# Gated linear attention's recurrence in chunks of 128 tokens instead of 64, decays within a chunk relative to its 64th token

## Chip, core and metric

The kernel runs on one core of a Trainium2 chip. The metric is the device time of one execution in microseconds: 1509.54 us is the median of three runs of the kernel before (1508.78 to 1512.38).

## What is computed

A decoder trunk of two layers on 512 tokens of width 1024. Layer 0 mixes with block-sparse attention and a gated MLP, layer 1 with gated linear attention; each layer then attends to 256 memory tokens and applies a feed-forward part. All inputs and outputs are float32. The change is in layer 1's mixer, with four heads, keys of 128 and values of 256 columns. With b the running sum of the log gates within a chunk, the reference computes it by chunks of 64 tokens:

```python
b = jnp.cumsum(log_a.astype(f32).reshape(Bn, H, nc, GLA_CHUNK, dk), axis=3)
b_last = b[:, :, :, -1:, :]
q_in = qc * jnp.exp(b)
k_in = kc * jnp.exp(-b)
att = jnp.where(causal, jnp.einsum('bhnid,bhnjd->bhnij', q_in, k_in), 0.0)
o_intra = jnp.einsum('bhnij,bhnjv->bhniv', att, vc)
k_state = kc * jnp.exp(b_last - b)
d_state = jnp.einsum('bhnjd,bhnjv->bhndv', k_state, vc)
...
def step(s_prev, xs):
    ds_n, dec_n = xs
    return dec_n[..., None] * s_prev + ds_n, s_prev
...
o_inter = jnp.einsum('bhnid,bhndv->bhniv', q_in, s_before)
```

The chunk's size is a matter of the algorithm only: with another one the sum of o_intra and o_inter is mathematically the same.

## The kernel before

Activations lie transposed, channels on the 128 partitions and 512 tokens along the free axis. Every float32 operand is split into a high half (`split`: a copy to float32r on ScalarE, L109, or with a scale L112) and a low half (the difference on VectorE, L110, or L113), and `mm3` makes each product of three TensorE matmuls: high x high (L132), high x low (L133), low x high (L134). `ws_tile` projects 128 output channels (24 wide matmuls of 512 columns), `gemm_as` projects tokens (L370 to L372).

Layer 1 runs by the tokens of a string, `GLA_ORDER`: z and g make the gates, Q0 to Q3 are `gla_qk` (queries and keys of a head), V0 and V1 the values of two heads, R0 to R3 the output gates, S0 to S3 `gla_core` (scores and recurrence), out the output projection, mem and k the memory keys of the next step. This is the order of the program. A scheduler then orders each engine's queue by its own timeline, so the projections of the next head (wide, into `ps_mm`, four banks) are woven among the narrow matmuls of `gla_core`. On the chip each engine runs its queue in that order.

`gate_decays` makes `bcum`, a scan along the tokens that is set back every 64 (L1378). `gla_qk` scales the queries by exp(b) and the keys by exp(-b), and makes the state's keys, scaled by exp(b_last - b) (`es`, transposed on TensorE by L137). The queries are laid in `qpH`, `qpL` with 64 zero columns between chunks, so that a query-state product over 128 columns of queries touches one chunk's half and adds zeros to the other.

`gla_core` computes the scores by tiles of 128 tokens (key x query, `ps_t`, 128 columns), keeps with `copy_predicated` what the mask `cmi` allows (two blocks of 64 on the diagonal), splits them, and runs eight chunks. An even chunk adds the intra-chunk product of its tile (256 columns); every chunk but the first adds the query-state product (`ps_t<-sH`, `ps_t<-sL`, 256 columns over 128 contraction rows); every chunk but the last makes the key-value product (`ps_s`, 256 columns, over the 64 contraction rows of its half), the new state `st` (L1476, L1478) and its halves `sH`, `sL`. The output is normed, transposed back, gated and split.

## Time and profile before

| | |
|---|---|
| median of three runs | 1509.54 us |
| profiled execution, its own time | 1511.11 us |
| its span, from the first to the last instruction | 1509.4 us |
| busy: TensorE, VectorE, ScalarE | 98%, 70%, 49% |
| mean granted TensorE clock | 0.996 of full speed |
| key-value products of the four heads | from 814.4 to 964 us of the span |

A busy share counts the time in which at least one instruction of the engine is under way. Matmuls are pipelined and their ends are modelled, so TensorE's pace is read from the distance between starts. A bracket in a timeline tells how long the engine was idle and what ended that.

### The profile page before, as it was taken

How to read it: one execution, taken by the hardware profiler on the slowest of the kernel's cores; microseconds unless marked ns; L12 is line 12 of the kernel's file. 1: busy time of each engine (PE TensorE's matmuls, PEld its weight loads, DVE VectorE, ACT ScalarE, POOL GpSimd, SP SyncE). 2: the span in 40 equal slices, each digit the busy share in tenths (PEclk: the TensorE clock that was granted, in tenths of full speed). 3: DMA queues.
4: the chain of work that ended last, by engine and by line, in shares of the span. 5: the costliest groups of instructions: out<-in, count | busy, mean ns of one | idle time of the engine just before them, and what ended most of it. 6: DMA issues, size and time to landing. Idle time of an engine off the chain costs nothing.

```text
span 1509.4 us, 18961 instructions
## 1 busy us (share of the span) xinstructions
PE 1483.3 (98%) x6982; PEld 1213.3 (80%) x6982; DVE 1060.7 (70%) x1873; ACT 742.5 (49%) x1304; POOL 84.5 (6%) x104
## 2 busy tenths in 40 slices
PE   8999999999999999999999999999999999999999
PEld 6787777788888888888687787888888888888877
DVE  6786866755889686786757556867568886877762
ACT  6546553553655353453535434555536553544551
POOL 4511100000000000000000000000000000000000
PEclk9999999999999999999999999999999999999999
DMA  7231331222432432415122222253214325323022
GB/s 218 84 98 57 125 110 58 78 65 68 142 95 77 154 94 88 126 43 162 43 64 77 70 70 70 78 160 112 71 57 145 99 71 160 105 71 119 28 84 98
DMA packets 144269, 143.22 MB, mean 95 GB/s; under 512 B 7532, under 2 KB 105952, under 8 KB 144176
## 3 DMA queue, kind: packets, MB, share of 16 engines
q1 hardware_dynamic: 142272, 140.53, 29.8%
q0 software_dynamic: 800, 1.37, 0.4%
q8 instruction: 55, 0.90, 0.2%
q14 instruction: 38, 0.31, 0.1%
q10 hardware_dynamic: 1104, 0.11, 0.1%
HBM read 139.88 MB, written 2.10 MB: 94 GB/s over the span
## 4 chain that ended last, share of the span: by engine, by line
PE 90%; DVE 3%; ACT 1%; issue 1%; POOL 1%; DMA 0%; ACTq 0%; POOLq 0%
PE ps_mm L132 12%; PE ps_mm L134 12%; PE ps_mm L133 12%; PE ps_mm L370 5%; PE ps_mm L372 5%; PE ps_s L466 5%; PE ps_mm L371 5%; PE ps_s L467 5%; PE ps_s L468 5%; PE ps_t L466 4%; PE ps_t L467 4%; PE ps_t L468 4%; PE ps_t L137 1%; PE ps_mm L137 1%; PE ps_s L132 1%; PE ps_t L132 1%
## 5 line engine op out<-in xcount | busy, mean ns | idle before, releaser
L109 ACT ACTIVATE wh<-raw 128x1024 fp32r<-128x1024 f32 x180 | 190.5, 1058 | 259.3 <-PE ps_mm L133 106.0
L110 DVE TENSOR_TENSOR wl<-raw,wh 128x1024 fp32r<-128x1024 f32 x180 | 221.0, 1228 | 114.5 <-ACT wh L109 106.9
L132 PE MATMUL ps_mm<-slot,wh 128*128 128x512 f32 x544 | 213.0, 396 | 4.0 <-ACT slot L109 2.1
L134 PE MATMUL ps_mm<-slot,wl 128*128 128x512 f32 x544 | 214.6, 395 | 0.0
L133 PE MATMUL ps_mm<-slot,wh 128*128 128x512 f32 x544 | 214.4, 394 | 0.0
L370 PE MATMUL ps_mm<-wh,slot 128*128 128x512 f32 x384 | 151.2, 398 | 2.8 <-DVE slot L900 1.3
L371 PE MATMUL ps_mm<-wh,slot 128*128 128x512 f32 x384 | 151.7, 396 | 0.0
L372 PE MATMUL ps_mm<-wl,slot 128*128 128x512 f32 x384 | 147.1, 394 | 0.1
L466 PE MATMUL ps_s<-wh,slot 128*128 128x512 f32 x320 | 126.4, 395 | 0.8
L467 PE MATMUL ps_s<-wh,slot 128*128 128x512 f32 x320 | 124.9, 390 | 0.0
L132 PEld LDWEIGHTS ps_mm<-slot,wh 128*128 128x128 f32 x544 | 103.1, 190 | 24.6 <-ACT slot L109 2.2
L134 PEld LDWEIGHTS ps_mm<-slot,wl 128*128 128x128 f32 x544 | 103.0, 189 | 21.4
L468 PE MATMUL ps_s<-wl,slot 128*128 128x512 f32 x320 | 119.6, 390 | 0.0
L133 PEld LDWEIGHTS ps_mm<-slot,wh 128*128 128x128 f32 x544 | 102.8, 189 | 20.6
L1237 DVE TENSOR_TENSOR slot<-ps_mm,slot 128x512 f32<-128x512 f32 x80 | 55.1, 690 | 64.4 <-PE ps_mm L134 63.5
L466 PE MATMUL ps_t<-wh,slot 128*128 128x512 f32 x240 | 94.4, 394 | 0.0
L467 PE MATMUL ps_t<-wh,slot 128*128 128x512 f32 x240 | 93.6, 390 | 0.0
L144 POOL TENSOR_TENSOR s<-s,mhalf 128x2 f32<-128x2 f32 (+3 forms) x46 | 52.1, 1135 | 680.3 <-DVE s L142 678.5
L468 PE MATMUL ps_t<-wl,slot 128*128 128x512 f32 x240 | 87.7, 394 | 0.0
L370 PEld LDWEIGHTS ps_mm<-wh,slot 128*128 128x128 f32 x384 | 72.3, 189 | 18.1 <-DVE slot L900 1.7
L372 PEld LDWEIGHTS ps_mm<-wl,slot 128*128 128x128 f32 x384 | 72.2, 188 | 14.5 <-DVE wl L110 0.5
L371 PEld LDWEIGHTS ps_mm<-wh,slot 128*128 128x128 f32 x384 | 72.5, 189 | 13.9
(342 smaller groups left out, 3018.2 us busy)
## 6 DMA issues: line engine op xcount, KB each, us to landing
raw<-in_ffn_w_gu SPq DMA_DIRECT2D x40, 512.0 KB, 3.6
raw<-in_xa_w_kv SPq DMA_DIRECT2D x32, 512.0 KB, 3.8
pt<-in_ffn_w_down SPq DMA_DIRECT2D x64, 256.0 KB, 3.1
raw<-in_od_w_in SPq DMA_DIRECT2D x24, 512.0 KB, 3.6
pt<-in_ffn_w_gu SPq DMA_DIRECT2D x40, 256.0 KB, 3.7
raw<-in_xa_w_q SPq DMA_DIRECT2D x16, 512.0 KB, 3.8
raw<-in_xa_w_out SPq DMA_DIRECT2D x16, 512.0 KB, 3.4
raw<-in_ev_w_in SPq DMA_DIRECT2D x12, 512.0 KB, 4.1
```

The source lines that it names most:

```text
L109: A.activation(h, src, AF.Copy)
L110: V.tensor_tensor(l, src, h.bitcast(F32), ALU.subtract)
L132: PE.matmul(ps, ah, bh, start=start, stop=False)
L133: PE.matmul(ps, ah, bl, start=False, stop=False)
L134: PE.matmul(ps, al, bh, start=False, stop=stop)
L370: PE.matmul(pss[t], a, wh[:, kk, :], start=st, stop=False)
L371: PE.matmul(pss[t], b, wh[:, kk, :], start=False, stop=False)
L372: PE.matmul(pss[t], a, wl[:, kk, :], start=False, stop=sp_)
L466: PE.matmul(acc[t], ah, h[:, i, :], start=st, stop=False, skip_group_check=True)
L467: PE.matmul(acc[t], al, h[:, i, :], start=False, stop=False, skip_group_check=True)
L468: PE.matmul(acc[t], ah, l[:, i, :], start=False, stop=sp_, skip_group_check=True)
L1237: V.tensor_tensor(xT[m], ps, xT[m], ALU.add)
```

## The change

The loop runs over four chunks of 128 tokens, and the scan is set back every 128 tokens. The queries are scaled by exp(b - b at the 64th token) for the scores (`qcH`, `qcL`) and by exp(b) for the state (`q0H`, `q0L`), the keys by exp(b at the 64th token - b) for the scores and by exp(b_last - b) for the state. The decay of the state is a small tile `dec` of four columns. The mask is a whole triangle of 128 x 128, made in a buffer of the `tmp` pool, and the layout with zero columns goes. A key-value product is over 128 contraction rows.

```diff
@@ -1320,13 +1320,15 @@
     sl.free(w2r)
-    cm = sp.tile([P, 2, 64], F32, tag="cm", name="cm", bufs=1)
-    G.memset(cm, 1.0)
-    G.affine_select(cm, cm, pattern=[[64, 2], [1, 64]], compare_op=ALU.is_ge, fill=0.0, base=0,
+    cm = tmp()
+    G.memset(cm[:, :P], 1.0)
+    G.affine_select(cm[:, :P], cm[:, :P], pattern=[[1, P]], compare_op=ALU.is_ge, fill=0.0, base=0,
                     channel_multiplier=-1)
-    V.memset(cm[0:64, 1, :], 0.0)
     cmi = cp.tile([P, P], I32, name="cmi")
-    V.tensor_copy(cmi, cm.rearrange("p a b -> p (a b)"))
+    V.tensor_copy(cmi, cm[:, :P])
     gv = [[None] * NT, [None] * NT]
     gvl = [[None] * NT, [None] * NT]
@@ -1354,7 +1356,7 @@
         V.tensor_copy(zst[64:80, :], zh[0:16, :].bitcast(F32))
     def gate_decays():
-        smask = sl.get((P, 8, 64))
+        smask = sl.get((P, NT, P))
         V.memset(smask, 1.0)
         V.memset(smask[:, :, 0:1], 0.0)
         smask2 = smask.rearrange("p c j -> p (c j)")
@@ -1381,31 +1383,28 @@
         sl.free(w2s, zst, smask)
     def gla_qk(hd):
-        b3 = bcum[hd].rearrange("p (c j) -> p c j", c=8)
+        b3 = bcum[hd].rearrange("p (t j) -> p t j", t=NT)
         psq = ws_tile(wv, hd * P, nm.h, nm.l)
         tq = tmp()
         V.tensor_tensor(tq, psq, nm.rb, ALU.mult)
         psk = ws_tile(wv, 512 + hd * P, nm.h, nm.l)
         tk = tmp()
         V.tensor_tensor(tk, psk, nm.rb, ALU.mult)
-        ep, em, es = sl.get(), tmp(tag="em", bufs=1), tmp(tag="es", bufs=1)
+        e0, em, es, ec = sl.get(), tmp(tag="em", bufs=1), tmp(tag="es", bufs=1), sl.get()
+        dec = small(NT)
+        for e, c in ((em, P // 2 - 1), (es, P - 1)):
+            V.tensor_tensor(e.rearrange("p (t j) -> p t j", t=NT), b3[:, :, c:c + 1].to_broadcast([P, NT, P]), b3,
+                            ALU.subtract)
         with tc.issue_after(hs["last"].ins):
-            A.activation(ep, bcum[hd], AF.Exp, scale=1.0 / 16)
-            A.activation(em, bcum[hd], AF.Exp, scale=-1.0 / 16)
-        V.scalar_tensor_tensor(tq, tq, 128.0 ** -0.5, ep, ALU.mult, ALU.mult)
-        qpH = [sl.get((P, 2, 192), F32R) for _ in range(2)]
-        qpL = [sl.get((P, 2, 192), F32R) for _ in range(2)]
-        for i in range(2):
-            for q_ in (qpH[i], qpL[i]):
-                G.memset(q_[:, :, 64:128].bitcast(F32), 0.0)
-            src = tq[:, i * MEM:(i + 1) * MEM].rearrange("p (t c j) -> p t c j", t=2, c=2)
-            dh = qpH[i].rearrange("p t (b j) -> p t b j", b=3)[:, :, 0:3:2, :]
-            dl = qpL[i].rearrange("p t (b j) -> p t b j", b=3)[:, :, 0:3:2, :]
-            A.activation(dh, src, AF.Copy)
-            V.tensor_tensor(dl, src, dh.bitcast(F32), ALU.subtract)
-        V.tensor_tensor(es.rearrange("p (c j) -> p c j", c=8), b3[:, :, 63:64].to_broadcast([P, 8, 64]), b3,
-                        ALU.subtract)
-        A.activation(es, es, AF.Exp, scale=1.0 / 16)
+            A.activation(e0, bcum[hd], AF.Exp, scale=1.0 / 16)
+            A.activation(dec, b3[:, :, P - 1], AF.Exp, scale=1.0 / 16)
+            A.activation(ec, em, AF.Exp, scale=-1.0 / 16)
+            A.activation(em, em, AF.Exp, scale=1.0 / 16)
+            A.activation(es, es, AF.Exp, scale=1.0 / 16)
+        for e in (ec, e0):
+            V.scalar_tensor_tensor(e, tq, 128.0 ** -0.5, e, ALU.mult, ALU.mult)
+        qcH, qcL = split_slots(ec)
+        q0H, q0L = split_slots(e0)
         V.tensor_tensor(em, em, tk, ALU.mult)
         kiH, kiL = split_slots(em)
         V.tensor_tensor(es, es, tk, ALU.mult)
@@ -1413,7 +1412,8 @@
         for t in range(NT):
             transpose(ps[:, t * P:(t + 1) * P], es[:, t * P:(t + 1) * P])
         ksH, ksL = split_slots(ps)
-        hs[hd] = ep, qpH, qpL, kiH, kiL, ksH, ksL
+        sl.free(e0, ec, bcum[hd])
+        hs[hd] = dec, qcH, qcL, q0H, q0L, kiH, kiL, ksH, ksL
     def gla_v(pr):
         def evac(t, ps):
@@ -1432,7 +1432,7 @@
         hs["r", hd] = rT
     def gla_core(hd):
-        ep, qpH, qpL, kiH, kiL, ksH, ksL = hs[hd]
+        dec, qcH, qcL, q0H, q0L, kiH, kiL, ksH, ksL = hs[hd]
         rT = hs["r", hd]
         vs = slice((hd % 2) * MEM, (hd % 2 + 1) * MEM)
         vh_, vl_ = gv[hd // 2], gvl[hd // 2]
@@ -1440,13 +1440,8 @@
         G.memset(att, 0.0)
         ps = ps_t()
         for t in range(NT):
-            i = t // 2
-            o = ps[:, t * P:(t + 1) * P]
-            def qv(q_):
-                return q_[i][:, t % 2, :].rearrange("p (b j) -> p b j", b=3)[:, 0:3:2, :]
-            mm3(o, kiH[:, t * P:(t + 1) * P], kiL[:, t * P:(t + 1) * P], qv(qpH), qv(qpL), True, True)
+            ts = slice(t * P, (t + 1) * P)
+            mm3(ps[:, ts], kiH[:, ts], kiL[:, ts], qcH[:, ts], qcL[:, ts], True, True)
         V.copy_predicated(att.rearrange("p (t i) -> p t i", t=NT), cmi.unsqueeze(1).to_broadcast([P, NT, P]),
                           ps.rearrange("p (t i) -> p t i", t=NT))
         atH, atL = split_slots(att)
@@ -1455,33 +1450,27 @@
         osb = []
         st, sH, sL = None, None, None
         pso = None
-        for c in range(8):
-            t, par = c // 2, c % 2
-            rs = slice(par * 64, par * 64 + 64)
-            if par == 0:
-                if t % 2 == 0:
-                    pso = ps_t()
-                o = pso[:, (t % 2) * MEM:(t % 2 + 1) * MEM]
-                mm3(o, atH[:, t * P:(t + 1) * P], atL[:, t * P:(t + 1) * P], vh_[t][:, vs], vl_[t][:, vs],
-                    True, False)
-            if c > 0:
-                ql = slice(par * 64, par * 64 + P)
-                mm3(o, qpH[t // 2][:, t % 2, ql], qpL[t // 2][:, t % 2, ql], sH, sL, False, par == 1)
-            if c < 7:
+        for t in range(NT):
+            ts = slice(t * P, (t + 1) * P)
+            if t % 2 == 0:
+                pso = ps_t()
+            o = pso[:, (t % 2) * MEM:(t % 2 + 1) * MEM]
+            mm3(o, atH[:, ts], atL[:, ts], vh_[t][:, vs], vl_[t][:, vs], True, t == 0)
+            if t > 0:
+                mm3(o, q0H[:, ts], q0L[:, ts], sH, sL, False, True)
+            if t < NT - 1:
                 psd = ps_s()
-                ks = slice(t * P, (t + 1) * P)
-                mm3(psd[:, :MEM], ksH[rs, ks], ksL[rs, ks], vh_[t][rs, vs], vl_[t][rs, vs], True, True)
+                mm3(psd[:, :MEM], ksH[:, ts], ksL[:, ts], vh_[t][:, vs], vl_[t][:, vs], True, True)
                 sn = tp.tile([P, MEM], F32, tag="st", name="st", bufs=2)
-                if c == 0:
+                if t == 0:
                     V.tensor_copy(sn, psd[:, :MEM])
                 else:
-                    V.scalar_tensor_tensor(sn, st, ep[:, c * 64 + 63:c * 64 + 64], psd[:, :MEM],
-                                           ALU.mult, ALU.add)
+                    V.scalar_tensor_tensor(sn, st, dec[:, t:t + 1], psd[:, :MEM], ALU.mult, ALU.add)
                 st = sn
                 sH = tp.tile([P, MEM], F32R, tag="sH", name="sH", bufs=2)
                 sL = tp.tile([P, MEM], F32R, tag="sL", name="sL", bufs=2)
                 split(sH, sL, sn)
-            if par == 1 and t % 2 == 1:
+            if t % 2 == 1:
                 ss = small(2)
                 for i in range(2):
                     jn = tmp(tag="tj", bufs=1)
@@ -1493,9 +1482,7 @@
                     V.tensor_scalar(os_[:, i * MEM:(i + 1) * MEM], pso[:, i * MEM:(i + 1) * MEM],
                                     ro[:, i:i + 1], None, ALU.mult)
                 osb.append(os_)
-        sl.free(*qpH)
-        sl.free(*qpL)
-        sl.free(ep, kiH, kiL, ksH, ksL, atH, atL, bcum[hd])
+        sl.free(qcH, qcL, q0H, q0L, kiH, kiL, ksH, ksL, atH, atL)
         for dv in range(2):
             ps = ps_t()
             for t in range(NT):
```

The excerpts below show how the queues change, in the rows' form line, operation, out<-in, shape.

On TensorE, in head 0's recurrence before: `ps_s` are key-value products over 64 rows, `ps_t<-sH` and `ps_t<-sL` query-state products, the other `ps_t` intra-chunk products.

```order
L132 MATMUL ps_s<-slot_364_7419,slot_358_7231 128x256
L133 MATMUL ps_s<-slot_365_7420,slot_358_7231 128x256
L134 MATMUL ps_t<-slot_362_7409,slot_372_7460 128x256
L132 MATMUL ps_t<-sH,slot_352_7206 128x256
L134 MATMUL ps_s<-slot_364_7419,slot_359_7232 128x256
L133 MATMUL ps_t<-sL,slot_352_7206 128x256
L134 MATMUL ps_t<-sH,slot_354_7208 128x256
L132 MATMUL ps_t<-slot_364_7419,slot_371_7459 128x256
L133 MATMUL ps_t<-slot_365_7420,slot_371_7459 128x256
L134 MATMUL ps_t<-slot_364_7419,slot_372_7460 128x256
L132 MATMUL ps_t<-sH,slot_352_7206 128x256
L133 MATMUL ps_t<-sL,slot_352_7206 128x256
```

The same place after:

```order
L132 MATMUL ps_mm<-slot_329_6979,wh 128x512
L133 MATMUL ps_mm<-slot_330_6980,wh 128x512
L134 MATMUL ps_t<-slot_363_7410,slot_373_7461 128x256
L132 MATMUL ps_t<-slot_365_7420,slot_372_7460 128x256
L133 MATMUL ps_t<-slot_366_7421,slot_372_7460 128x256
L134 MATMUL ps_t<-slot_365_7420,slot_373_7461 128x256
L132 MATMUL ps_t<-sH,slot_355_7217 128x256
L133 MATMUL ps_t<-sL,slot_355_7217 128x256
L134 MATMUL ps_t<-sH,slot_356_7218 128x256
L134 MATMUL ps_t<-slot_367_7430,slot_373_7461 128x256
```

Key-value products (`ps_s`) stood among the query-state products, and none does now; two chunks' reads of the state follow each other.

On VectorE, at head 0's start before, from the subtraction for `es` (L1406) to the first low half of a value tile (L113), with scans (L1378), weight splits (`wl`), the queries' product (L1395) and the keys' (L1409, L1411):

```order
L1406 TENSOR_TENSOR es<-slot_347_7123 128x512
L110 TENSOR_TENSOR wl<-raw,wh 128x1024
L1376 SCALAR_TENSOR_TENSOR slot_345_7110<-slot_345_7110,slot_346_7111 128x512
L1378 SCALAR_TENSOR_TENSOR slot_349_7129<-slot_338_7087,slot_343_7104 128x512
L1395 SCALAR_TENSOR_TENSOR tmp<-tmp,slot_351_7200 128x512
L1409 TENSOR_TENSOR em<-em,tmp 128x512
L1411 TENSOR_TENSOR es<-es,tmp 128x512
L110 TENSOR_TENSOR wl<-raw,wh 128x1024
L1378 SCALAR_TENSOR_TENSOR slot_350_7132<-slot_338_7087,slot_345_7110 128x512
L113 SCALAR_TENSOR_TENSOR slot_363_7410<-ps_mm,s_7020,slot_362_7409 128x512
```

The same place after; the subtractions are L1396, the queries' products L1405, the scans L1380, the keys' products L1410 and L1408:

```order
L1396 TENSOR_TENSOR em<-slot_347_7122 128x512
L1396 TENSOR_TENSOR es<-slot_347_7122 128x512
L110 TENSOR_TENSOR wl<-raw,wh 128x1024
L1378 SCALAR_TENSOR_TENSOR slot_345_7109<-slot_345_7109,slot_346_7110 128x512
L1380 SCALAR_TENSOR_TENSOR slot_349_7128<-slot_338_7086,slot_343_7103 128x512
L1405 SCALAR_TENSOR_TENSOR slot_351_7199<-tmp,slot_351_7199 128x512
L1405 SCALAR_TENSOR_TENSOR slot_352_7202<-tmp,slot_352_7202 128x512
L110 TENSOR_TENSOR wl<-raw,wh 128x1024
L1410 TENSOR_TENSOR es<-es,tmp 128x512
L1380 SCALAR_TENSOR_TENSOR slot_350_7131<-slot_338_7086,slot_345_7109 128x512
L1408 TENSOR_TENSOR em<-em,tmp 128x512
L113 SCALAR_TENSOR_TENSOR slot_364_7411<-ps_mm,s_7020,slot_363_7410 128x512
```

One subtraction and one product of the queries more stand ahead of L113, and a weight split ahead of the product for `es`.

On ScalarE, where the last head ends and the memory tokens of the next step begin (squares of `pp`, L521; L112 `slot<-ps_s,pc` their high halves), before:

```order
L1488 ACTIVATE tj,s_8673<-ps_t 128x256
L112 ACTIVATE slot_447_8917<-ps_s,pc 128x256
L109 ACTIVATE sH<-st 128x256
L112 ACTIVATE slot_447_8917<-ps_s,pc 128x256
L112 ACTIVATE slot_449_8928<-ps_s,pc 128x256
L1488 ACTIVATE tj,s_8734<-ps_t 128x256
L112 ACTIVATE slot_449_8928<-ps_s,pc 128x256
L1488 ACTIVATE tj,s_8734<-ps_t 128x256
L112 ACTIVATE slot_451_8947<-ps_s,pc 128x256
L521 ACTIVATE tj,s_8902<-pp_49_8904 128x512
L109 ACTIVATE wh<-raw 128x1024
L112 ACTIVATE slot_451_8947<-ps_s,pc 128x256
```

And after (L1477 are the squares of the recurrence's output, L109 `slot<-slot` the high halves of the gated output):

```order
L1477 ACTIVATE tj,s_8533<-ps_t 128x256 x2
L521 ACTIVATE tj,s_8701<-pp_49_8703 128x512
L521 ACTIVATE tj,s_8702<-pp_50_8704 128x512
L521 ACTIVATE tj,s_8701<-pp_51_8733 128x512
L521 ACTIVATE tj,s_8702<-pp_52_8734 128x512
L109 ACTIVATE wh<-raw 128x1024
L112 ACTIVATE slot_451_8716<-ps_s,pc 128x256
L112 ACTIVATE slot_453_8727<-ps_s,pc 128x256
L109 ACTIVATE slot_447_8551<-slot_440_8411 128x512
L112 ACTIVATE slot_451_8716<-ps_s,pc 128x256
L109 ACTIVATE slot_449_8561<-slot_441_8445 128x512
```

The high halves of the memory tokens stood among the state's halves `sH` and ahead of the squares of `pp`; now they come behind four squares and a weight split.

## Rows read from the trace of the kernel before

**Rows 1.** Page: busy time by engine, and the chain's shares by engine:

```profile
PE 1483.3 (98%) x6982; PEld 1213.3 (80%) x6982; DVE 1060.7 (70%) x1873; ACT 742.5 (49%) x1304; POOL 84.5 (6%) x104
...
PE 90%; DVE 3%; ACT 1%; issue 1%; POOL 1%; DMA 0%; ACTq 0%; POOLq 0%
```

**Rows 2.** TensorE's timeline, head 0: start us, duration, engine, line, out<-in, rows*columns, shape:

```profile
831.73 0.39 PE L132 MATMUL ps_mm<-slot,wh 128*128 128x512 f32 x1
831.96 0.39 PE L133 MATMUL ps_mm<-slot,wh 128*128 128x512 f32 x1
832.28 0.38 PE L132 MATMUL ps_s<-slot,slot 64*128 64x256 f32 x1
832.50 0.28 PE L133 MATMUL ps_s<-slot,slot 64*128 64x256 f32 x1
832.71 0.38 PE L132 MATMUL ps_t<-sH,slot 128*128 128x256 f32 x1
...
833.67 0.28 PE L132 MATMUL ps_t<-sH,slot 128*128 128x256 f32 x1
833.79 0.28 PE L133 MATMUL ps_t<-sL,slot 128*128 128x256 f32 x1
...
834.46 0.27 PE L134 MATMUL ps_s<-slot,slot 64*128 64x256 f32 x1
834.67 0.50 PE L134 MATMUL ps_mm<-slot,wl 128*128 128x512 f32 x1
835.01 0.40 PE L132 MATMUL ps_mm<-slot,wh 128*128 128x512 f32 x1
```

**Rows 3.** TensorE's groups by form, 760 to 1010 us: busy us, mean ns:

```profile
L132 PE MATMUL ps_s<-slot,slot 64*128 64x256 f32 x28 | 9.2, 382 | 0.6 <-DVE st L1476 0.6
...
L133 PE MATMUL ps_s<-slot,slot 64*128 64x256 f32 x28 | 6.7, 277 | 0.0
...
L132 PE MATMUL ps_t<-slot,slot 128*128 128x256 f32 x16 | 4.6, 294 | 0.0
```

**Rows 4.** TensorE's timeline in head 3's recurrence:

```profile
957.86 0.38 PE L134 MATMUL ps_s<-slot,slot 64*128 64x256 f32 x2 [0.61 <-DVE slot L110]
958.79 0.39 PE L132 MATMUL ps_s<-slot,slot 64*128 64x256 f32 x1 [0.55 <-DVE st L1476]
```

**Rows 5.** TensorE's timeline at head 0's start; brackets: idle time, releaser:

```profile
803.00 0.39 PE L372 MATMUL ps_mm<-wl,slot 128*128 128x512 f32 x1
804.07 0.66 PE L137 MATMUL ps_t<-ident,es 128*128 128x128 f32 x4 [0.68 <-DVE es L1411]
804.72 0.33 PE L132 MATMUL ps_t<-slot,slot 128*128 128x128 f32 x1
806.98 0.50 PE L132 MATMUL ps_mm<-slot,wh 128*128 128x512 f32 x1 [1.94 <-DVE slot L113]
```

**Rows 6.** Timeline there: VectorE, and a table load of ScalarE:

```profile
802.15 0.67 DVE L1395 SCALAR_TENSOR_TENSOR tmp<-tmp,slot 128x512 f32<-128x512 f32 x1
802.73 0.68 DVE L1409 TENSOR_TENSOR em<-em,tmp 128x512 f32<-128x512 f32 x1
...
806.20 0.72 DVE L113 SCALAR_TENSOR_TENSOR slot<-ps_mm,s,slot 128x512 fp32r<-128x512 f32 x1
...
797.12 1.28 ACT L1393 ACT_TABLE_LOAD   x1
```

**Rows 7.** Windows: stretch, length, busy us by engine, PEclk, DMA share, GB/s:

```profile
806.00:812.00 6.00, 5.02 (x15) 3.99 (x16) 6.00 (x11) 3.04 (x6) 0.20 (x1) 0.72 0.31 87
```

**Rows 8.** ScalarE's and VectorE's timelines at the memory tokens:

```profile
970.23 1.07 ACT L109 ACTIVATE wh<-raw 128x1024 fp32r<-128x1024 f32 x1
...
971.34 1.23 DVE L110 TENSOR_TENSOR wl<-raw,wh 128x1024 fp32r<-128x1024 f32 x1
972.48 0.48 DVE L113 SCALAR_TENSOR_TENSOR slot<-ps_s,pc,slot 128x256 fp32r<-128x256 f32 x1
...
976.25 0.74 DVE L1504 SCALAR_TENSOR_TENSOR slot<-ps_t,pc,slot 128x512 f32<-128x512 f32 x1
```

## Prediction

> **What bounds the kernel now.** I read the page's first part, then its chain of waits, then the stretch of the gated-attention layer in time order. TensorE is busy 98% of the span, and 90% of the chain that ended last is TensorE; VectorE stands at 70%, ScalarE at 49% [rows 1]. So a microsecond of matmul issue is worth a microsecond of time, as long as the matmuls that replace it don't wait. Waits are rare: between 780 and 1010 us, where this layer runs, there are two places, one at its start and one in its last head (terms 6 and 5).
>
> Busy times of matmuls overlap, so they are no price. The price of a matmul is the distance from its start to the next start, and the timeline of head 0 shows it [rows 2]. A matmul of 512 columns is followed after 0.23 us (831.73 to 831.96), one of 256 columns over 128 rows after 0.12 us (833.67 to 833.79). A state product over 64 rows also takes 0.12 us by itself, but a change between 64 and 128 contraction rows is paid on both sides: the last matmul ahead of it is followed after 0.32 instead of 0.23 us (831.96 to 832.28), the first behind it after 0.22 instead of 0.12 (832.28 to 832.50). On the way back it is 0.21 (832.50 to 832.71, and 834.46 to 834.67) and, for a wide one, 0.34 instead of 0.23 (834.67 to 835.01). One change thus costs 0.09 + 0.10 to 0.11, about 0.195 us. The grouped rows say the same in durations: the state products over 64 rows, 84 of them, have a mean of 382 ns for the first of a triple, which stands behind most changes, and 277 ns for the second, against 294 ns for a product over 128 rows with as many columns [rows 3].
>
> **The change part by part.** All sums are made on the profiled execution, whose span of 1509.4 us is shorter by 1.7 us than its own time of 1511.11; the median of the runs is 1509.54.
>
> (1) Query times state. Seven chunks of a head read a state before, three do now, three matmuls each: over four heads 84 become 36, all of 256 columns over 128 rows. 48 x 0.12 us [rows 2] = 5.7 us, all on TensorE's queue, which sets the end: gain 5.7.
>
> (2) Key times value. 84 matmuls over 64 rows become 36 over 128 rows. In the timeline of the four heads 14 of the 84 start within 0.03 us of another on the other half of the rows (the row at 957.86 that stands for two is such a pair [rows 4]), so they cost 70 x 0.117 = 8.2 us. The new ones have no row of their own; the row nearest is the query-state product of the same shape, 0.12 us [rows 2]: 36 x 0.12 = 4.3. Gain 3.9. Bounds: 0.6 (had all 84 gone in pairs: 42 x 0.117 less 4.3) to 5.5 (had none).
>
> (3) Changes of contraction height. The 84 stand in 31 runs between matmuls over 128 rows (counted in the timeline, the first at 814.39, the last at 963.59 us), so 62 changes. No matmul of this layer is over 64 rows any more. 62 x 0.195 = 12.1 us gain. This is the largest term, and it is nowhere in the diff's arithmetic.
>
> (4) Scores and intra-chunk products keep number and columns (48 of 128, 48 of 256 columns): nothing. The query operand is contiguous now; the old strided one already ran at the pace of the contiguous.
>
> (5) Last head's waits. Before, the state products of head 3 stand nearly without wide matmuls between them, and TensorE is idle 0.61 us for a low half of the keys and 0.55 us for the release of a state bank [rows 4]. In the new order 21 wide ones (21 x 0.23 = 4.8 us) lie between its scores and its intra-chunk product, where before nine narrow ones did. Gain 1.2.
>
> (6) Head 0's start, a loss. TensorE sits from 803.2 to 806.98, with only five small matmuls in between, until VectorE has made the low half of the first value tile and so released a bank [rows 5]; VectorE works through its queue without a gap up to that instruction at 806.20 [rows 6]. The diff of VectorE's order puts two more ahead of it: the subtraction for em, and a second scaled product of the query. Two such start 0.58 us apart [rows 6], so the release comes 1.2 us later. ScalarE's new exponentials stand ahead of VectorE's use of them and don't end last. Loss 1.2; bounds 0 (something else of VectorE's queue moved) and 3.0 (a second stretch at half clock: TensorE was granted 0.72 of its clock in the 6 us around this idle time, that is about 3.4 us at 1.2 GHz [rows 7], which costs 1.7 us, and I leave that once, as before).
>
> (7) The hand-over to the memory keys, a loss. Before, the transposes of the memory tokens and their splits are woven into the last head's recurrence. Now that recurrence is done early, and in ScalarE's order four squares and a weight split stand ahead of the first split of the memory. The weight split can start only when the last out-projection matmul has freed its buffer; behind it follow, on VectorE, the low half of the weights, a gain product and the low half of the memory. From rows of the same instructions that is 1.07 for the split, 1.14 from the low half's start to the next, 0.74 for the gain product and 0.48 for the last [rows 8], some 3.5 us with the hand-overs, while TensorE has fourteen transposes and two wide matmuls, 2.0 us. Then the third group of transposes waits for a bank behind two more splits, about 0.7. Loss 2.2; bounds 0 (the weights come early enough) and 4.
>
> (8) Nothing: the mask on POOL (now made behind the layer's norm, still ahead of head 0's scores), sixteen zero fills that go, two more table loads on ScalarE at heads 2 and 3, one more exponential, and wider splits of the queries. VectorE and ScalarE lose sixteen state updates and splits in exchange and have 30% and 51% idle [rows 1]; were that cover gone, a table load of 1.28 us [rows 6] would be the price each time. The DMA queue's order is the same row for row. A few rows of the first 35 us swap places; between -0.5 and 0.5.
>
> Sum: 5.7 + 3.9 + 12.1 + 1.2 - 1.2 - 2.2 = 19.5 us. 1509.4 - 19.5 = 1489.9 of span, and from the median 1509.5 - 19.5 = 1490.0 us.
>
> **The rivals.** *The halves were hidden.* Products on the two halves of the rows can run side by side. The Trainium skill (TensorE: Matmul & The Clock Gate, Part 3: Packing small matmuls — row/col tiling) advises slicing a short contraction so that each part lands in its own row group and runs at the same time, which speaks against merging two halves into one. By rows: if the 84 had all run in pairs and the distances at a change belonged to something that stays (the bank, the reload of weights), terms 2 and 3 would be 0.6 and 0, and the sum 5.7 + 0.6 - 2.2 = 4.1, or 1505 us. For it: 14 of them do pair. Against it: most of them stand alone in their run, and [rows 2] shows ordinary changes of tile and bank at 0.12 us. 5%.
>
> *The recurrence is uncovered.* Twelve times (three a head) a query-state product needs a state that has gone through VectorE, ScalarE and VectorE. In the new order between 12 and 30 wide matmuls, some 3 us or more, stand between the state product and its use, but VectorE's queue holds 1.2 us weight splits in between. If half of the twelve waited 1 us, with one more stretch at half clock (1.7 us), 1498 us. 13% for 1495 to 1505.
>
> *Slower.* The same mechanism at its full price, at the same twelve places: TensorE arrives before the chain has begun, and each time stands through a weight split (1.14), the update, the high half and the low half (about 0.5 each, an estimate from the nearest row, 0.48) and the hand-overs, 2.8 us [rows 8]. 12 x 2.8 = 34 against the 21.7 of terms 1 to 3: 1522 us. It decides from 1.8 us a place (21.7 / 12). Against it: the count of wide matmuls above. 3%.
>
> *More.* Terms 6 and 7 don't come, and part of the 3 us of idle time at head 0 goes: 1482 to 1485. 5%.
>
> **How the numbers follow.** My forecast, 1485 to 1495, has 74%. Its lower end is 1490 without losses 6 and 7 and with the best of term 2 (1.2 + 2.2 + 1.6 = 5.0), the upper one has both losses at their upper bounds (1.8 + 1.8) and a part of what term 2 can lose. For 8 in 10 I take in the nearer half of the uncovered recurrence: 1485 to 1498. A measurement of this kernel can tell about 0.3%, 4.5 us, from no change. Faster by more: 74 + 13 + 5 and about half of the hidden halves, 95%. Within: 2%. Slower: 3%.
>
> **What would show each step.** In the profile after: no matmul over 64 rows between 780 and 990 us and 36 state products with a mean near 290 ns (terms 2 and 3); starts of state and query-state products 0.12 us apart with wide ones at 0.23 on both sides (3); idle time of TensorE at about 803 us of some 5 us instead of 3.8 (6); an idle place of 1.5 us behind the memory transposes, ended by VectorE's low half (7); no idle place in the last head's recurrence (5). The prediction is wrong if waits for the state's halves add up to more than 5 us, or if wide matmuls next to state products still take 0.32 us.

## Result and the profile after

The changed kernel takes 1493.51 us (median of 4 runs, 1491.76 to 1495.34) beside 1509.19 us for the kernel before on the same chip (4 runs): a ratio of 0.9886, 95% interval 0.9872 to 0.9900, so 1.1% faster. Forecast were 1490.0 us, in a range of 1485 to 1498. The profiled execution took 1494.02 us, 1492.3 of it span: 17.1 us less than before. The page's first part and the chain of waits of the changed kernel, as in [rows 1]:

```profile
PE 1462.1 (98%) x6886; PEld 1201.8 (81%) x6886; DVE 1054.9 (71%) x1848; ACT 744.5 (50%) x1298; POOL 83.2 (6%) x88
...
PE 89%; DVE 4%; ACT 1%; DMA 1%; issue 1%; POOL 0%; ACTq 0%; DVEq 0%
```

TensorE still bounds the kernel (98% busy; 89% of the chain, 90% before). Where the 17.1 us come from is read by cutting both timelines of TensorE at the same matmuls:

| from | to | before, us | after, us | change | forecast |
|---|---|---|---|---|---|
| start | last matmul ahead of the wait at 66 us | 66.28 | 65.80 | -0.5 | 0 |
| there | the first layer's attention (181.4 before) | 115.11 | 117.97 | **+2.9** | 0 |
| there | first projection of the gated layer (729.2) | 547.79 | 548.16 | +0.4 | 0 |
| there | head 0's idle place (803.0) | 73.83 | 73.77 | -0.1 | 0 |
| there | its end: head 0's idle place itself | 3.98 | 5.19 | +1.2 | +1.2 |
| there | last wide matmul ahead of the wait at 1457 | 650.34 | 629.34 | **-21.0** | -20.7 |
| there | last matmul (1505.3 before) | 47.96 | 47.96 | 0.0 | 0 |

From the last matmul to the end of the span it is another 4.1 us in both. The two lines on the gated layer came as worked out: -19.8 against -19.5. What was missed is in the first 180 us, where the change has only a mask: 2.4 us net.

TensorE's timeline around a state product of the changed kernel (start us, duration, engine, line, out<-in, rows*columns, shape), the counterpart of [rows 2]:

```profile
827.35 0.39 PE L132 MATMUL ps_mm<-slot,wh 128*128 128x512 f32 x1
827.58 0.28 PE L132 MATMUL ps_s<-slot,slot 128*128 128x256 f32 x1
827.69 0.28 PE L133 MATMUL ps_s<-slot,slot 128*128 128x256 f32 x1
827.81 0.28 PE L134 MATMUL ps_s<-slot,slot 128*128 128x256 f32 x1
827.93 0.40 PE L133 MATMUL ps_mm<-slot,wh 128*128 128x512 f32 x1
```

The product now runs over 128 rows. The last wide matmul ahead is followed after 0.23 us (827.35 to 827.58), not 0.32; the first product after 0.11, not 0.22. By groups (780 to 990 us; busy us, mean ns) the 36 products have lost the long mean of the first of a triple, 382 ns in [rows 3]:

```profile
L132 PE MATMUL ps_s<-slot,slot 128*128 128x256 f32 x12 | 3.4, 288 | 0.0
...
L133 PE MATMUL ps_s<-slot,slot 128*128 128x256 f32 x12 | 3.3, 283 | 0.0
```

What TensorE waits for between 780 and 1010 us (total us, times, longest):

```profile
PE ps_t L137 <- DVE es L1410: 2.4, 1, 2.4
PE ps_mm L132 <- DVE slot L113: 1.7, 1, 1.7
PE ps_mm L371 <- DVE slot L113: 1.2, 1, 1.2
PE ps_s L137 <- issue: 0.5, 1, 0.5
PE ps_mm L370 <- ACT wh L109: 0.3, 1, 0.3
```

No row names a state or one of its halves; the two waits of the last head in [rows 4] are gone. The first two rows are head 0's start, the third and fourth the hand-over to the memory keys.

### The profile page after: what moved, and what is told of

The parts are those of the page before. It is cut to its first block, busy times and chain, and to the rows that moved or that the text cites. A ratio compares the mean times of both kernels' runs of the same rounds, so it can differ in the third digit from the quotient of the medians.

```text
span 1492.3 us, 18677 instructions
## 1 busy us (share of the span) xinstructions
PE 1462.1 (98%) x6886; PEld 1201.8 (81%) x6886; DVE 1054.9 (71%) x1848; ACT 744.5 (50%) x1298; POOL 83.2 (6%) x88
## 4 chain that ended last, share of the span: by engine, by line
PE 89%; DVE 4%; ACT 1%; DMA 1%; issue 1%; POOL 0%; ACTq 0%; DVEq 0%
PE ps_mm L132 12%; PE ps_mm L134 12%; PE ps_mm L133 12%; PE ps_s L466 5%; PE ps_s L467 5%; PE ps_s L468 5%; PE ps_mm L372 5%; PE ps_mm L370 5%; PE ps_mm L371 5%; PE ps_t L466 4%; PE ps_t L467 4%; PE ps_t L468 4%; PE ps_t L137 1%; PE ps_mm L137 1%; DVE wl L110 1%; PE ps_mm L1120 1%
## 5 line engine op out<-in xcount | busy, mean ns | idle before, releaser
L109 ACT ACTIVATE wh<-raw 128x1024 fp32r<-128x1024 f32 x180 | 190.4, 1058 | 250.8 <-PE ps_mm L133 86.3
L370 PEld LDWEIGHTS ps_mm<-wh,slot 128*128 128x128 f32 x384 | 72.8, 190 | 19.5 <-DVE slot L900 2.9
```

What stands on the lines that cost most here:

```text
L109: A.activation(h, src, AF.Copy)
L370: PE.matmul(pss[t], a, wh[:, kk, :], start=st, stop=False)
```

## The experiments

Times are medians beside the kernel before on the same chip. Its runs there were longer and more scattered (1509.1 to 1516.9 us in the first group of experiments, much the same in the others), so medians tell 2 us badly. What decides is the distance between the same two matmuls of a trace, which repeats to some 0.5 us once the stretches at half clock in it are counted. In such a stretch TensorE's clock is at its lower level, 1.2 of 2.4 GHz, and wide matmuls (512 columns) start 0.43 us apart instead of 0.23, so each costs 0.20 us more. "The core" below is the stretch from the first wide matmul behind head 0's idle place to the last one ahead of the wait at 1457 us (1440 in the changed kernel): 650.34 us before, 629.34 after, and 628.83 in a second trace of the changed kernel, taken with the last experiments (5 matmuls at half clock in both; the first has a wait of 0.3 us at 993 us that the second lacks).

**Is the change of contraction height the price? Put back.** Of each key-value product only the first 64 rows are taken:

```
-    mm3(psd[:, :MEM], ksH[:, ts], ksL[:, ts], vh_[t][:, vs], vl_[t][:, vs], True, True)
+    mm3(psd[:, :MEM], ksH[0:64, ts], ksL[0:64, ts], vh_[t][0:64, vs], vl_[t][0:64, vs], True, True)
```

> The changed kernel, but each key-value product of the recurrence takes only the first 64 of a chunk's 128 rows (the other half of the sum is left out). Number, columns and order of all instructions on every engine stay as in the changed kernel; the 36 products stand in 13 runs between matmuls over 128 rows, so 26 changes of contraction height come back. Theory (a change of height costs TensorE about 0.195 us, the same 256 columns cost 0.12 us over 64 or 128 rows): +26 x 0.195 = +5.1 us against the changed kernel's 1493.5, so 1498.6, with 0.32 us instead of 0.23 from the last wide matmul to the next start and 0.22 instead of 0.12 behind the first product. Rival (what made these places dear was switching between the two halves of the rows, or banks, or the number of products): all products are on one half here, so 0, or 1493.5, and starts of 0.12 and 0.23 us as in the changed kernel.

Measured: 1501.74 us, ratio 0.9926 (0.9906 to 0.9946), where the changed kernel has 0.9886. The core takes 634.49 us, 5.15 more than in the first trace of the changed kernel and 5.66 more than in the second, with as many matmuls at half clock in it (5) and no wait at 993 us. Forecast were 5.1. TensorE's timeline:

```profile
829.14 0.39 PE L132 MATMUL ps_mm<-slot,wh 128*128 128x512 f32 x1
829.46 0.38 PE L132 MATMUL ps_s<-slot,slot 64*128 64x256 f32 x1
829.68 0.28 PE L133 MATMUL ps_s<-slot,slot 64*128 64x256 f32 x1
829.80 0.27 PE L134 MATMUL ps_s<-slot,slot 64*128 64x256 f32 x1
830.00 0.50 PE L133 MATMUL ps_mm<-slot,wh 128*128 128x512 f32 x1
```

From the wide matmul 0.32 us (829.14 to 829.46), from the first product 0.22, from the second 0.12, from the third 0.20, and the wide one behind it 0.34 to the next (830.00 to 830.34 in the trace). All products lie on the same half of the rows, so it is not a change of half that costs, and their number and columns are the same. 5.15 / 26 = 0.198 us a change of height by the first trace, 5.66 / 26 = 0.218 by the second; 0.195 stood in the prediction.

**Taken away in the kernel before.** All 84 products over 128 rows, with nothing else of the change:

```
-            rs = slice(par * 64, par * 64 + 64)
+            rs = slice(0, P)
```

> The kernel before, with one edit: each of its 84 key-value products contracts over all 128 rows of a tile instead of one half of 64 (so each state takes in both 64-token chunks of the tile, and what it computes is another sum). Nothing else of the change is in it: still seven states a head, and the same number of matmuls. Theory (the change of height is the price): the 62 changes go, -62 x 0.195 = -12.1 us, and 14 pairs that ran side by side no longer do, +14 x 0.12 + 70 x 0.003 = +1.9 us, so -10.2, or 1499.3 us; with between -9 and -12 taken as agreeing, since the order of a few matmuls of the last head moves as well. Rival (halves were hidden beside each other and the gain came from the smaller number of products alone): +1.9 us or more, 1511.4.

Measured: 1503.66 us, ratio 0.9928 (0.9907 to 0.9949), -0.72% or 10.9 us of the 1513.11 of before there. The core takes 640.83 us, 9.51 less than before (7 matmuls at half clock in either). 0.3 us of that are shorter waits of the last head, where the order moved a little. So this one line brings about half of the gain, though it makes TensorE contract twice as many rows. The groups over 128 rows, to be held against 382 and 277 ns in [rows 3]:

```profile
L132 PE MATMUL ps_s<-slot,slot 128*128 128x256 f32 x28 | 8.0, 291 | 0.4 <-DVE st L1476 0.4
...
L133 PE MATMUL ps_s<-slot,slot 128*128 128x256 f32 x28 | 7.8, 282 | 0.0
```

The rival that the halves ran hidden beside each other asked for 1511.4 us and is out. The Trainium skill (TensorE: Matmul & The Clock Gate, Part 3: Packing small matmuls — row/col tiling) advises slices of the rows that run at the same time. Here 28 of the 84 did, in 14 pairs, and the trace shows what the 84 together paid: 9.5 us more than over the full height.

**The start: is it the mask?** The kernel before, with its own mask made in a work tile, so late:

```
-    cm = sp.tile([P, 2, 64], F32, tag="cm", name="cm", bufs=1)
-    G.memset(cm, 1.0)
...
+    cm = tmp()
+    G.memset(cm[:, :P], 1.0)
...
```

> The kernel before, in which only the mask moves: it is built in a work tile as in the changed kernel, so POOL makes it behind the norm of the gated layer and not at 20 us, while its content (64-token blocks) stays. This gives the first 120 rows of TensorE, VectorE and ScalarE the order that they have in the changed kernel. Theory (the 2.4 us that the changed kernel has lost by 180 us come from this new order: TensorE's wait at 66 us for VectorE's L900 grows from 1.3 to 2.5 us, and a stretch at half clock follows): +2.4 us, 1511.9, with the granted clock low at about 70 us and the gated layer's first matmul later by 2.4 to 2.7 us. Rival (the late start of the changed kernel is one execution's, not the order's): no change, 1509.5, and the wait at 66 us is 1.3 us.

and the changed kernel, with its mask made in a tile of its own, so early:

```
-    cm = tmp()
-    G.memset(cm[:, :P], 1.0)
...
+    cm = sp.tile([P, P], F32, tag="cm", name="cm", bufs=1)
+    G.memset(cm, 1.0)
...
```

> The changed kernel, with its 128-token mask built in a tile of its own as the kernel before does it, so that POOL makes it at about 20 us and VectorE converts it there. Theory (the order of the first 120 rows is what costs): the wait at 66 us is 1.3 us again, no stretch at half clock at 70 us, and the time falls by 2.4 us from 1493.5 to 1491.1; the gated layer itself unchanged. Rival (one execution's accident): 1493.5, with the wait and the half clock at 70 us in some executions of either order.

Measured: the first 1515.57 us, ratio 1.0012 (0.9999 to 1.0024), the second 1490.91, ratio 0.9855 (0.9837 to 0.9874). The first ratio alone doesn't exclude 1, and the second's interval overlaps that of the changed kernel; the traces decide. TensorE ahead of and behind the wait, first in the kernel before:

```profile
66.28 0.39 PE L370 MATMUL ps_mm<-wh,slot 128*128 128x512 f32 x1
67.95 0.50 PE L370 MATMUL ps_mm<-wh,slot 128*128 128x512 f32 x1 [1.29 <-DVE slot L900]
```

In the changed kernel:

```profile
65.80 0.39 PE L370 MATMUL ps_mm<-wh,slot 128*128 128x512 f32 x1
68.66 0.50 PE L370 MATMUL ps_mm<-wh,slot 128*128 128x512 f32 x1 [2.47 <-DVE slot L900]
...
69.75 0.63 PE L371 MATMUL ps_mm<-wh,slot 128*128 128x512 f32 x1
```

In the kernel before with the late mask:

```profile
66.76 0.39 PE L370 MATMUL ps_mm<-wh,slot 128*128 128x512 f32 x1
69.97 0.50 PE L370 MATMUL ps_mm<-wh,slot 128*128 128x512 f32 x1 [2.83 <-DVE slot L900]
```

In the changed kernel with the early mask:

```profile
65.34 0.39 PE L370 MATMUL ps_mm<-wh,slot 128*128 128x512 f32 x1
66.66 0.50 PE L370 MATMUL ps_mm<-wh,slot 128*128 128x512 f32 x1 [0.93 <-DVE slot L900]
```

With the early mask TensorE waits 1.29 and 0.93 us for VectorE's L900, with the late mask 2.47 and 2.83, whichever recurrence the kernel has. From the last matmul ahead of the wait to the attention of that layer it is 115.1 and 114.8 us against 118.0 and 118.3. In the changed kernel the row of 0.63 us behind the wait begins a stretch of seven wide matmuls at half clock (0.43 us apart, not 0.23), 1.4 us on top of a wait that is 1.2 us longer. The mask itself is no cost where it is now made: it is converted at 774.4 us and first read at 824.2. What costs is that its two early instructions on VectorE and two on POOL went out of the queues at 20 to 30 us, and that the scheduler put other instructions in another order into the place; in the traces VectorE's order differs as late as 58 us. Which of the two costs was not separated. VectorE's L900, in the kernel before and then in the changed kernel:

```profile
67.21 0.68 DVE L900 TENSOR_TENSOR slot<-ps_mm,rb 128x512 f32<-128x512 f32 x1
```

```profile
67.92 0.68 DVE L900 TENSOR_TENSOR slot<-ps_mm,rb 128x512 f32<-128x512 f32 x1
```

It starts 0.93 us behind the last matmul ahead of the wait (66.28 to 67.21) in the first, 2.12 behind it (65.80 to 67.92) in the second. When TensorE reaches the place is no matter of the order: 65.3 to 67.4 us in the seven traces with the late mask, 65.3 to 67.1 in the five with the early one. The wait is: 2.37 to 2.83 us in the seven, 0.20 to 1.62 in the five.

**Head 0's start.** First, both added VectorE instructions moved to POOL, with the factor of the query moved into an earlier instruction (that line is not shown):

```
-            V.tensor_tensor(e.rearrange(...), ...)
+            (G if e is em else V).tensor_tensor(e.rearrange(...), ...)
...
-            V.scalar_tensor_tensor(e, tq, 128.0 ** -0.5, e, ALU.mult, ALU.mult)
+            (V if e is ec else G).tensor_tensor(e, tq, e, ALU.mult)
```

> The changed kernel, with the two instructions that the change added to VectorE's queue ahead of head 0's first value tile given to POOL in all four heads: the subtraction that makes em, and the second scaled product of the query (the factor 128^-0.5 goes into the query's scaling, so VectorE's count is otherwise the same). Theory (term 6: these two, 0.6 us each, are the 1.2 us by which TensorE's idle place at head 0's start grew from 3.98 to 5.19 us): the place shrinks to about 4.0 us and the time by 1.2 us. Rival (VectorE's queue isn't what ends last there now, but the chain over ScalarE's exponentials and em, or POOL slows VectorE beside it): 5.2 us or more, no gain, and if POOL's em comes late the scores of a head wait, +1 us or more a head.

Measured: 1497.74 us, ratio 0.9908 (0.9887 to 0.9928), an interval that overlaps that of the change by itself. The trace shows a loss where a gain was expected: the idle place grew from 5.19 to 6.49 us, and 4.0 were forecast. TensorE's two waits there, then VectorE's timeline, then POOL's:

```profile
PE ps_mm L132 <- DVE slot L113: 2.6, 1, 2.6
PE ps_t L137 <- DVE es L1410: 2.6, 1, 2.6
```

```profile
800.92 2.07 DVE L1380 TENSOR_TENSOR_SCAN slot<-slot,slot 128x512 f32<-128x512 f32 x1
802.92 1.72 DVE L1396 TENSOR_TENSOR es<-slot 128x512 f32<-128x512 f32 x1
```

```profile
800.57 1.34 POOL L1396 TENSOR_TENSOR em<-slot 128x512 f32<-128x512 f32 x1 [25.50 <-DVE slot L1380]
802.49 1.59 POOL L1405 TENSOR_TENSOR slot<-tmp,slot 128x512 f32<-128x512 f32 x1 [0.58 <-ACT slot L1399]
```

The subtraction at 802.92 took 1.72 us, where its twin in the changed kernel took 0.69, and the scan at 800.92 took 2.07 instead of 1.22. Each ended about its usual duration after POOL's instruction did: the scan at 802.99, 1.08 us after 801.91 (800.57 + 1.34), the subtraction at 804.64, 0.56 us after 804.08 (802.49 + 1.59). So they stood while POOL worked, and VectorE lost 1.9 us to save 1.2. The Trainium skill (SBUF — State Buffer, section "SBUF: two separate sides") says that a VectorE instruction with two inputs in SBUF and a GpSimd (POOL) instruction that reads SBUF lock each other out for the whole of an instruction. The trace agrees, with the times above. But the order also put the weight split behind the product for es, and a low half of the query ahead of the value tile's low half, so this run doesn't settle term 6. The next one is clean: only the second query product is moved, behind the scores, and the difference of VectorE's order ahead of the release is that one row.

```
-        for e in (ec, e0):
-            V.scalar_tensor_tensor(e, tq, 128.0 ** -0.5, e, ALU.mult, ALU.mult)
+        V.scalar_tensor_tensor(ec, tq, 128.0 ** -0.5, ec, ALU.mult, ALU.mult)
...
+        with tc.issue_after(cpy.ins):
+            V.scalar_tensor_tensor(e0, tq, 128.0 ** -0.5, e0, ALU.mult, ALU.mult)
+        q0H, q0L = split_slots(e0)
```

> The changed kernel, with the second scaled product of the query (that for the state, 0.58 us on VectorE) made behind the head's scores, in gla_core, and not in gla_qk. On VectorE's queue this takes exactly one instruction away ahead of head 0's transposes and of the low half of the first value tile; POOL is left alone. Theory (term 6: TensorE's idle place at head 0's start ends when VectorE's queue comes to that low half): both the transposes and the low half come 0.6 us earlier and the place shrinks from 5.19 to about 4.6 us, with VectorE's subtractions back at their 0.68 us, which were 1.72 us beside POOL. In the heads behind it the state products of the query come later by one or two instructions of VectorE, which is hidden: total -0.6 us. Rival (the place is set by ScalarE's exponentials or by the projection's loads): 5.2 us as before; or the later product makes the query-state products wait, 0.5 us or more a head.

Measured: the idle place is 4.58 us, 0.61 less. The whole time is 1492.69 us, ratio 0.9867 (0.9849 to 0.9885), whose interval is far too wide for 0.6 us. TensorE's waits there, against 2.4 and 1.7 in the changed kernel:

```profile
PE ps_t L137 <- DVE es L1408: 1.8, 1, 1.8
PE ps_mm L132 <- DVE slot L113: 1.7, 1, 1.7
```

**The hand-over to the memory keys.** The preparation of the memory goes ahead of the last head's scores:

```
-GLA_ORDER = "z g Q0 R0 V0 S0 Q1 R1 S1 Q2 V1 R2 S2 Q3 R3 free S3 out mem k k k k k k"
+GLA_ORDER = "z g Q0 R0 V0 S0 Q1 R1 S1 Q2 V1 R2 S2 Q3 R3 free mem S3 out k k k k k k"
```

> The changed kernel with one word of the layer's order moved: the preparation of the memory tokens and their keys stands ahead of the last head's scores and recurrence, not behind the out-projection. Theory (term 7: TensorE waits 1.4 and 0.6 us at the hand-over because the squares, the weight split and the splits of the memory come in a row behind the recurrence): with the recurrence woven between them those idle places (at 947.6 and 950.5 us in the changed kernel) go, -2.0 us, and no new one above 0.5 us comes in the last head. Rival (the last head's recurrence then stands without the out-projection's wide matmuls as cover, as in the kernel before, or the freed place shows up at the next hand-over): the gain is eaten by waits for the states' halves, 0 to +2 us.

Measured: 1491.29 us, ratio 0.9863 (0.9847 to 0.9879). The core takes 627.39 us with 6 matmuls at half clock, against 629.34 and 628.83 with 5 in the two traces of the changed kernel: -1.95 and -1.44, or -2.15 and -1.64 with the clock set equal. The interval of the ratio overlaps that of the changed kernel, so the traces decide. TensorE's waits from 780 to 1010 us:

```profile
PE ps_t L137 <- DVE es L1410: 2.4, 1, 2.4
PE ps_mm L132 <- DVE slot L113: 1.7, 1, 1.7
PE ps_mm L372 <- DVE wl L110: 0.5, 1, 0.5
```

The waits at 947 and 950 us are gone, the last head's recurrence has none, and a new one of 0.5 us stands at a low half of the key weights.

**Three edits together**, with POOL for head 0's start and then with the late query product in its place; and the changed kernel again, unedited, beside the latter:

> The changed kernel with three edits together: the mask early in a tile of its own, the two VectorE instructions on POOL, the memory's preparation ahead of the last head's scores. Theory (the three places are independent and all on TensorE's queue): -2.9 (the wait at 66 us and the half clock behind it) -1.2 -2.0 = -6.1 us against the changed kernel, a ratio to the kernel before of 0.9845 against the changed kernel's 0.9886. Rival (one of the places gives its gain back later): the early mask alone, -2.9, ratio 0.987.

> The changed kernel with the mask early, the memory's preparation ahead of the last head's scores, and the second scaled query product behind the scores. Theory: -2.9 (order of the first rows) -2.0 (hand-over to the memory) -0.6 (head 0's start) = -5.5 us against the changed kernel beside it. Rival (one gain is given back in another place, as with POOL): -3 us.

> The changed kernel itself, unedited, on the same chip, as the measure for the two others: 0.9886 of the kernel before; theory and rival expect the same of it. Its trace also tells what differs between two executions of one program: the idle places at 66, 805 and 947 us should come back within 0.2 us if they belong to the order, and the number and places of the stretches at half clock may differ.

Measured: with POOL 1491.26 us, ratio 0.9868 (0.9849 to 0.9887), where 0.9845 was expected: POOL takes 1.3 us more at head 0 (6.50 us) instead of giving 1.2. With the late query product 1488.79 us, ratio 0.9842 (0.9824 to 0.9860); the changed kernel beside it 1496.15, ratio 0.9889 (0.9873 to 0.9905). The last two intervals don't meet: the version with three edits beats both kernels, by 0.47% the changed one and by 1.6% the one before. The medians are 7.4 us apart where 5.5 were expected; part of that may be the clock (below). The waits that it has left between 780 and 1010 us are those of head 0, 1.8 and 1.7 us, as with the late query product alone.

## Why the prediction was right

**(1) to (3), 21.7 us: right in sum and in mechanism.** The core fell by 21.0 us, 0.4 of it since two matmuls fewer ran at half clock. Added to the 20.6 that remain: 2.0 for the hand-over and 0.4 for the short wait of 0.3 us and its restart at 993 us, which work against it; taken off: 1.2 for the last head's waits. That leaves 21.8 for the three terms. The second trace of the changed kernel, without the wait at 993 us, gives 21.9 in the same way. The two experiments on the height show term 3 from both sides: 0.198 to 0.218 us a change put back, and, taken away, 9.2 us without the waits; with the 1.9 us that the lost pairs cost by the prediction's rows, (9.2 + 1.9) / 62 = 0.18 us. Terms 1 and 2 weren't run by themselves; what speaks for them is that all 120 matmuls of 256 columns of the recurrence cost 14.3 us, 0.119 each. By difference, the core of the kernel before with all products over 128 rows is 11.5 us longer than that of the changed kernel (640.83 - 629.34). With the same corrections (the clock, the hand-over, the wait at 993 us and the 0.9 us of waits that the last head still has there) that is 12.6, of which 1.9 are the lost pairs. So this split gives 10.7 to terms 1 and 2 and 11.1 to term 3, where 9.6 and 12.1 were forecast. Put back, 62 changes at 0.198 to 0.218 would be 12.3 to 13.5. The sum is shown; how it divides is known to 1 or 2 us.

**(4), nothing: right.** The scores keep 0.11 us from start to start.

**(5), 1.2 us: right.** No row of the waits is in the last head's recurrence.

**(6), a loss of 1.2: right, in a form that was not quite foreseen.** TensorE's idle place at head 0's start:

```profile
805.70 0.39 PE L372 MATMUL ps_mm<-wl,slot 128*128 128x512 f32 x1
808.51 0.66 PE L137 MATMUL ps_t<-ident,es 128*128 128x128 f32 x4 [2.42 <-DVE es L1410]
810.89 0.80 PE L132 MATMUL ps_mm<-slot,wh 128*128 128x512 f32 x1 [1.72 <-DVE slot L113]
```

It is 5.19 us (805.70 to 810.89) against 3.98 in [rows 5]. VectorE there, where "x2" at 805.45 are the two scaled products of the query:

```profile
805.45 1.27 DVE L1405 SCALAR_TENSOR_TENSOR slot<-tmp,slot 128x512 f32<-128x512 f32 x2
806.64 1.22 DVE L110 TENSOR_TENSOR wl<-raw,wh 128x1024 fp32r<-128x1024 f32 x1
807.77 0.69 DVE L1410 TENSOR_TENSOR es<-es,tmp 128x512 f32<-128x512 f32 x1
808.38 1.22 DVE L1380 TENSOR_TENSOR_SCAN slot<-slot,slot 128x512 f32<-128x512 f32 x1
809.51 0.67 DVE L1408 TENSOR_TENSOR em<-em,tmp 128x512 f32<-128x512 f32 x1
810.09 1.40 DVE L113 SCALAR_TENSOR_TENSOR slot<-ps_mm,s,slot 128x512 fp32r<-128x512 f32 x2
```

The queue has no gap until 809.5, and the product for es, which frees the transposes, stands behind the two query products and a weight split. So the extra instructions lengthen the wait ahead of the transposes, from 0.7 to 2.4 us; the second wait, for the low half of the value tile, stayed (1.9 before, 1.7 after). One instruction taken off VectorE's queue gave back 0.61 us of the 1.21, as the sum said; the other, the subtraction for em, wasn't taken off alone. A second stretch at half clock, the upper bound, did not come; the one there had 7 wide matmuls before and 5 after, and 11 in the changed kernel with the early mask.

**(7), a loss of 2.2: right.** The two places cost 2.0 us, and go with the order of the memory, which gave back 1.6 to 2.2. The first wait, 1.2 us, ends with VectorE's low half as foreseen. The second, for which the prediction named a bank behind two splits, is put down to nothing that the profile shows ("issue", 0.5); whether it was the bank stays open.

**(8), between -0.5 and 0.5: wrong.** This is the step that failed: "a few rows of the first 35 us swap places". The exchange was seen in the order and priced at nothing, since it lies ahead of any work of the gated layer. From the last matmul ahead of the place to the attention it cost 2.9 us: 1.2 on a wait that the profile of before already had at 66 us, with no cover at all, 1.4 in a stretch at half clock behind it, and 0.3 in small differences. Since this execution reached the place 0.5 us sooner, 2.4 remain by 180 us. The step should have asked which wait of TensorE follows next behind the swapped rows and whether it ends with one of the engines that were re-ordered. In total it was the third of TensorE's waits for VectorE in that trace.

The other 0.4 us are at a wait for VectorE at 728 us. There VectorE's L1179 stands behind a weight split, and the high half that the split needs, which ScalarE begins when a DMA has landed, began 0.91 instead of 0.53 us behind the start of TensorE's transposes. This wait is 1.13 to 1.16 us in the five traces with the early mask and 1.21 to 1.64 in the seven with the late one; why the load comes later was not settled. The span exceeds its forecast of 1489.9 by 2.4 us, which is the sum of these places (-0.5 + 2.9 + 0.4, and -0.4 in the rest). That the time stayed within the range is owed to room that was left for terms 2, 6 and 7, not for this. One reading in this term was off without effect: the traces have 17 table loads against 16, one more and not two, and TensorE waits for none.

**The rivals.** Hidden halves: refuted by the runs on the height, above all by the one over the full height. An uncovered recurrence, and its full form as the slower case: no wait for a state in any of the traces of the changed kernel. "More", 1482 to 1485: terms 6 and 7 did come. Even the three edits' ratio of 0.9842 gives only 1485.3 us on the 1509.19 of before.

## What to carry to other kernels

Price a small matmul by the distance from its start to the next, on both sides of it, and look at how often neighbours change their contraction height: here about 0.2 us a change made a product over half the rows dearer than the same over all of them, and one changed slice brought half of this gain. When an edit drops or adds an instruction anywhere in a program that a scheduler orders, follow the engines whose rows swap to the next wait of the bounding engine, even if the edit's own stage is far behind it. Before work goes from VectorE to an idle POOL, look at whether VectorE's instructions beside it take longer.

## What was not expected of the hardware

**Stretches at half clock come and go between executions of one program.** Of the changed kernel two executions were profiled. Two windows of the first (window, length, busy us, granted clock, DMA share, GB/s), then of the second:

```profile
60.00:80.00 20.00, 17.53 (x75) 0.91 0.31 96
260.00:280.00 20.00, 16.83 (x77) 0.91 0.09 26
```

```profile
60.00:80.00 20.00, 17.33 (x75) 0.91 0.31 92
260.00:280.00 20.00, 16.83 (x82) 1.00 0.13 37
```

At 260 to 280 us both have the same idle places (the longest 2.07 us), and one runs at full clock throughout. The changed kernel with the memory early waited even longer at 70 us than either, and kept its clock:

```profile
70.66 0.50 PE L370 MATMUL ps_mm<-wh,slot 128*128 128x512 f32 x1 [2.83 <-DVE slot L900]
```

```profile
60.00:80.00 20.00, 17.17 (x80) 1.00 0.35 105
```

Of the seven profiled executions with the late mask (six programs) five have the stretch behind that wait and two don't; of the five with the early mask, whose waits are shorter, none has. Each stretch there is five to eight wide matmuls at 0.43 instead of 0.23 us, 1.0 to 1.6 us. Over a run they add up: the unedited changed kernel took 1497.4 us at a mean granted clock of 0.993 and 1491.9 at 0.997. The clock that is lost, 0.007 x 1495.7 - 0.003 x 1490.2 = 6.0 us by the spans (an estimate from rounded clocks), is about the 5.5 by which the times differ. What decides whether a wait is followed by a stretch was not settled: the length of the wait alone is not it.

**VectorE took longer while POOL worked**, in the two places shown above: 0.69 became 1.72 us for a subtraction, 1.22 became 2.07 for a scan, beside POOL instructions of 1.34 and 1.59 us.
